# Eight wide matmuls and then eight narrow ones, in place of turns

## The chip, the cores and the metric

The kernel runs on one core of one Trainium2 chip. The metric is the device time of one execution in microseconds. The program is written in Python against a tile framework. Each engine (TensorE for matmuls, VectorE, ScalarE, GpSimd and SyncE) has a queue of its own, which it works off in order; a planner decides in which order the instructions enter the queues, from the order of the program, priorities and its own estimate of when things are ready, and it puts in the waits.

## The reference

The reference is one encoder layer over 512 positions of 2048 channels, in float32. A normed input is projected into two groups (a convolution module and a neighbourhood attention), these are normed and projected back, and a gated MLP follows. The part that matters here is the MLP's first step:

```python
xn = rms_norm(x, ffn_norm_g[l])
up = jnp.einsum("bsd,df->bsf", xn, w_up[l])          # (512 x 2048) by (2048 x 11264)
up = depthwise_conv(up, ffn_dw_w[l], ffn_dw_b[l])    # width 3
gate, val = jnp.split(up, 2, axis=-1)                # 5632 each
x = x + jnp.einsum("bsf,fd->bsd", jax.nn.silu(gate) * val, w_down[l])
```

## The kernel before

**Exactness.** TensorE is fed in a rounded 32-bit form. A float32 weight tile (`raw`, 128 x 1024, eight slices of 128 x 128) is split by `parts` into `whi`, a rounded copy that ScalarE makes (L125), and `wlo`, the remainder that VectorE makes (L126). Activations are split in the same way. A product is then the sum of three: high by high, high by low, low by high.

**Stages.** In order of time: the input projection (tiles `pj`, with the attention's matmuls between), the output projection (`po`), the up projection (`pu`, from about 702 to 1578 us) and the down projection (`pd`). `mm3` issues the three matmuls of a slice in turn (L138 and L141 with a slice of `whi`, L142 with the same slice of `wlo`). In the input and output projection all three have 512 columns. The down projection does its three at L819 to L821, each of 512 columns too, and there the weights are what moves.

**The up projection.** It works on 44 units `f` of 128 gate and 128 value columns. The 2 x 2 block product of a unit (halves of the channels by halves of the positions) is done with seven block products in place of eight, each with a sum or difference of weights and one of activations; `c` numbers them, and `TURN = (3, 2, 4, 5, 1, 0, 6)` is their order. The activations of all seven stand ready in `comb[c][k]`, for the eight slices k of 128 channels: a tile of 512 columns of which the first 256 (`H`) are the high part of the 256 positions and the last 256 the low part. So one matmul of `whi` with the whole tile gives high by high in the left half of the accumulator and high by low in the right half, and one matmul of 256 columns adds `wlo` by the high part to the left half. After the product, `folded` adds the halves (ScalarE L707, VectorE L708), or `copied` (ScalarE L704) copies the accumulator into another one on which a further product goes on.

Six of the seven products are made of these pairs, 16 matmuls each: L694 with 512 columns, L697 with 256. The product with c = 2 runs through `mm3` with halves of the tile, as 24 matmuls of 256 columns. An accumulator is one PSUM bank of 512 columns; a product's sixteen matmuls all add into the same one.

**What sets the order around it.** `weights()` is called at the start of a product; it makes the weights of the product three further on (`AHEAD = 3`, with `NW = 4` buffers for each of whi and wlo), which puts their loads on SyncE's queue, and up to eight products ahead (`FAR = 8`) it issues the two weight sums of a unit, as a load on SyncE's queue and an adding transfer on GpSimd's (L643). When all matmuls of a product are issued, `tick` lets pending steps follow the last one, and `done`, here `paced`, lets GpSimd issue transfers behind the last matmul of the fourth product (`ws`, sums of down weights, L191 and L194). `pin` keeps the first matmul of a product in the order of the program (from the second unit on); all others the planner places. The results of a unit pass through the width-3 convolution and the gate on ScalarE and VectorE, and go to DRAM for the down projection (L754) until the last units, which stay.

Of the kernel before, what the change touches and what calls it, by code (L numbers as in the profile page):

```python
# [16 lines left out]
P = 128  # L17
D = 2048
S = 512
# [15 lines left out]
U = 8  # L35
# [5 lines left out]
H = S // 2  # L41
# [31 lines left out]
def layer(ctx: ExitStack, tc: tile.TileContext, xT, xn, w_in, w_out, w_up, w_down, par, tab, g3, out):  # L73
    nc = tc.nc
# [8 lines left out]
    @contextmanager  # L83
    def shifted(by):

        at = tc.cur_priority
        tc.cur_priority = max(at + by, 0)
        yield
        tc.cur_priority = at + (tc.cur_priority - max(at + by, 0))

    def t2(name, dt=F32):
        return tp.tile([P, S], dt, tag="t2k", name=name)
# [17 lines left out]
    ps = psm.tile([P, S], F32, tag="mm", name="warm")  # L110
# [7 lines left out]
    def raw_unit(src, n):  # L118
        raw = t4([P, U * P], "raw")
        return raw, nc.sync.dma_start(raw[:, :n], src)  # L120

    def parts(raw, n):
        hi = wpool.tile([P, U * P], F32R, tag="whi", name="whi", bufs=NW)
        lo = wpool.tile([P, U * P], F32R, tag="wlo", name="wlo", bufs=NW)
        i = nc.scalar.activation(hi[:, :n], raw[:, :n], AF.Copy)  # L125
        j = nc.vector.tensor_sub(lo[:, :n], raw[:, :n], hi[:, :n].bitcast(F32))  # L126
        return hi, lo, i, j
# [5 lines left out]
    tight = []  # L133

    def mm3(ps, w, wk, mh, ml, start, stop, more=False):
        hi, lo = w[:2]
        a = slice(wk * P, (wk + 1) * P)
        i = nc.tensor.matmul(ps, hi[:, a], mh, start=start, stop=False, skip_group_check=more)  # L138
        if tight:
            pin(i)  # L140
        nc.tensor.matmul(ps, hi[:, a], ml, start=False, stop=False, skip_group_check=more)  # L141
        return nc.tensor.matmul(ps, lo[:, a], mh, start=False, stop=stop, skip_group_check=more)  # L142
# [4 lines left out]
    def tick(behind):  # L147
        for todo in (steps, asteps):
            while todo:
                try:  # L150
                    with tc.issue_after(behind.ins):
                        next(todo[0])
                    break
                except StopIteration:
                    todo.pop(0)
# [5 lines left out]
    def weights():  # L161
        at = weights.at
        weights.at += 1
        for i in range(at, min(at + 1 + FAR, len(plan))):
            if i in sums:
                sums.pop(i)()
        while len(made) < min(at + 1 + AHEAD, len(plan)):
            made.append(plan[len(made)]())
        return made[at]
# [81 lines left out]
    pin = tc.keep_in_program_order  # L251
# [24 lines left out]
    for j, n in enumerate((NC_, 0)):  # L276
        raw, i = raw_unit(w_in[n, :, U * P:2 * U * P], U * P)
        pin(i)
        w = parts(raw, U * P)
# [9 lines left out]
    for step in ORDER:  # L289
        i = next(a_ if step == "a" else q_)  # L290
# [238 lines left out]
    p, n = -1, 0  # L529
# [51 lines left out]
    comb = [[] for _ in range(7)]  # L581
# [103 lines left out]
    def up(f, done):  # L685

        def product(c, ps, more):
            hi, lo = wt = weights()
            for k in range(U):
                m, w = comb[c][k], slice(k * P, (k + 1) * P)  # L690
                if c == 2:
                    i = mm3(ps[:, :H], wt, k, m[:, :H], m[:, H:], k == 0, k == U - 1)
                    continue
                i = nc.tensor.matmul(ps, hi[:, w], m, start=k == 0 and not more, stop=False, skip_group_check=more)  # L694
                if k == 0 and tight:
                    pin(i)
                i = nc.tensor.matmul(ps[:, :H], lo[:, w], m[:, :H], start=False, stop=k == U - 1,  # L697
                                     skip_group_check=more)
            tick(i)
            done(TURN.index(c), i)  # L700

        def copied(to, ps):
            with shifted(-100):
                nc.scalar.activation(to, ps, AF.Copy)  # L704

        def folded(to, ps):
            nc.scalar.activation(to, ps[..., H:], AF.Copy)  # L707
            add(to, to, ps[..., :H])  # L708

        product(3, pa, False)  # L710
        tight[:] = [1] * (f > 0)
        copied(pd_, pa)
        product(2, pc_, False)
        w = t2("w")[:, :H]
        nc.scalar.activation(w, pc_[:, :H], AF.Copy)
        product(4, pa, True)
        copied(pe, pa)
        product(5, pd_, True)
        g = t2("g")
        folded(g[:, :H], pd_)  # L720
        product(1, pa, True)
        copied(pb, pa)
        product(0, pe, True)
        v = t2("vl")
        by = v.rearrange("p (i t) -> p i t", i=2)
        folded(by[:, 1], pa)
        folded(by[:, 0], pe)
        add(by, by, w.unsqueeze(1).broadcast_to([P, 2, H]))
        product(6, pb, True)
        folded(g[:, H:], pb)  # L730
        return g, v
# [269 lines left out]
```

## Time and profile before

| | us |
|---|---|
| median of 3 runs | 2015.14 (2013.87 to 2018.29) |
| the profiled execution | 2016.07 |
| its span, first to last instruction | 2014.3 |
| TensorE busy in it | 1994.4 |
| VectorE busy | 1599.6 |
| ScalarE busy | 1105.2 |
| mean granted TensorE clock | 0.997 |
| DMA moved | 451.01 MB, 224 GB/s |

The span is what the trace shows; what the execution took beyond it lies ahead of the first instruction and behind the last. In the profile PE stands for TensorE's matmuls, PEld for its weight loads, which run beside the matmuls, DVE for VectorE, ACT for ScalarE, POOL for GpSimd, SP for SyncE. Matmuls are pipelined: each is shown with a length that overlaps the next one's, so a matmul's price is the distance from its start to the next start. The chain of waits assigns every stretch of time on the path that ends last to one instruction, and for a stream of matmuls that is this distance.

### The profile page before, as it was taken

How to read it: one execution, taken by the hardware profiler on the slowest of the kernel's cores; microseconds unless marked ns; L12 is line 12 of the kernel's file. 1: busy time of each engine (PE TensorE's matmuls, PEld its weight loads, DVE VectorE, ACT ScalarE, POOL GpSimd, SP SyncE). 2: the span in 40 equal slices, each digit the busy share in tenths (PEclk: the TensorE clock that was granted, in tenths of full speed). 3: DMA queues.
4: the chain of work that ended last, by engine and by line, in shares of the span. 5: the costliest groups of instructions: out<-in, count | busy, mean ns of one | idle time of the engine just before them, and what ended most of it. 6: DMA issues, size and time to landing. Idle time of an engine off the chain costs nothing.

```text
span 2014.3 us, 28373 instructions
## 1 busy us (share of the span) xinstructions
PE 1994.4 (99%) x10525; PEld 1685.5 (84%) x10525; DVE 1599.6 (79%) x2296; ACT 1105.2 (55%) x1729; POOL 226.1 (11%) x310
## 2 busy tenths in 40 slices
PE   9999999999999999999999999999999999999998
PEld 7878888877788888888888888888888788888886
DVE  5994798498547888888888888888888798886765
ACT  7234423448525676666666666666666645554654
POOL 0110111110001111111111111111110400000000
PEclk9999999999999999999999999999999999999999
DMA  9677767776858879998999999999986976666563
GB/s 341 167 218 181 177 170 202 183 182 199 256 147 220 203 206 263 244 267 235 265 240 258 253 253 251 251 256 248 258 239 170 375 229 212 218 212 195 191 210 114
DMA packets 143114, 451.01 MB, mean 224 GB/s; under 512 B 15232, under 2 KB 23936, under 8 KB 141568
## 3 DMA queue, kind: packets, MB, share of 16 engines
q1 hardware_dynamic: 90608, 293.98, 43.6%
q0 software_dynamic: 42624, 148.92, 34.2%
q10 hardware_dynamic: 9744, 6.30, 1.0%
q8 instruction: 82, 1.34, 0.3%
q14 instruction: 56, 0.46, 0.1%
HBM read 430.27 MB, written 111.15 MB: 269 GB/s over the span
## 4 chain that ended last, share of the span: by engine, by line
PE 94%; DMA 2%; DVE 2%; ACT 1%; issue 0%; SPq 0%; DVEq 0%; ACTq 0%
PE pu L694 25%; PE pu L697 12%; PE pd L821 7%; PE pd L819 7%; PE pd L820 7%; PE pj L138 6%; PE pj L141 6%; PE pj L142 6%; PE po L138 3%; PE po L141 3%; PE po L142 3%; PE pu L141 2%; PE pu L138 2%; PE pu L142 2%; DVE y L367 1%; DMA xn<-in_xn 1%
## 5 line engine op out<-in xcount | busy, mean ns | idle before, releaser
L125 ACT ACTIVATE whi<-raw 128x1024 fp32r<-128x1024 f32 x572 | 605.5, 1059 | 722.4 <-PE pj L141 211.7
L126 DVE TENSOR_TENSOR wlo<-raw,whi 128x1024 fp32r<-128x1024 f32 x572 | 699.0, 1223 | 304.1 <-ACT whi L125 274.9
L694 PE MATMUL pu<-xc,whi 128*128 128x512 f32 x2112 | 748.2, 399 | 0.0
L697 PE MATMUL pu<-xc,wlo 128*128 128x256 f32 x2112 | 593.1, 281 | 0.0
L694 PEld LDWEIGHTS pu<-xc,whi 128*128 128x128 f32 x2112 | 396.8, 188 | 96.9 <-issue 0.2
L697 PEld LDWEIGHTS pu<-xc,wlo 128*128 128x128 f32 x2112 | 399.0, 189 | 0.3 <-issue 0.2
L138 PE MATMUL pj<-xh,whi 128*128 128x512 f32 x624 | 246.8, 398 | 1.4 <-DVE gate L352 1.4
L142 PE MATMUL pj<-xh,wlo 128*128 128x512 f32 x624 | 243.7, 390 | 0.8 <-DVE wlo L126 0.8
L141 PE MATMUL pj<-xl,whi 128*128 128x512 f32 x624 | 244.4, 392 | 0.1
L821 PE MATMUL pd<-whi,ho 128*128 128x512 f32 x616 | 240.1, 391 | 4.0 <-DVE ho L777 4.0
L819 PE MATMUL pd<-whi,ho 128*128 128x512 f32 x616 | 240.5, 391 | 0.5 <-ACT ho L776 0.5
L820 PE MATMUL pd<-wlo,ho 128*128 128x512 f32 x616 | 240.4, 390 | 0.0
L367 DVE SCALAR_TENSOR_TENSOR y<-ch,prm,y 128x507 f32<-128x507 f32 (+14 forms) x240 | 169.9, 742 | 3.2
L194 POOL DMA_DIRECT2D ws<-in_w_down x88 | 79.4, 902 | 568.1 <-DMA ws<-ws 279.0
L138 PEld LDWEIGHTS pj<-xh,whi 128*128 128x128 f32 x624 | 117.5, 188 | 30.2 <-issue 3.5
L821 PEld LDWEIGHTS pd<-whi,ho 128*128 128x128 f32 x616 | 116.0, 188 | 29.3 <-DVE ho L777 5.3
L142 PEld LDWEIGHTS pj<-xh,wlo 128*128 128x128 f32 x624 | 117.5, 188 | 26.1 <-DVE wlo L126 1.3
L141 PEld LDWEIGHTS pj<-xl,whi 128*128 128x128 f32 x624 | 117.7, 189 | 24.0 <-DVE xl L257 0.5
L819 PEld LDWEIGHTS pd<-whi,ho 128*128 128x128 f32 x616 | 115.9, 188 | 25.1 <-ACT ho L776 0.9
L820 PEld LDWEIGHTS pd<-wlo,ho 128*128 128x128 f32 x616 | 116.1, 188 | 24.6 <-DVE wlo L126 0.3
L643 POOL DMA_DIRECT2D raw<-in_w_up x88 | 85.2, 968 | 344.6 <-DMA raw<-in_w_up 85.6
L138 PE MATMUL pu<-xc,whi 128*128 128x256 f32 x352 | 99.7, 283 | 0.5 <-ACT xc L586 0.5
(185 smaller groups left out, 2524.4 us busy)
## 6 DMA issues: line engine op xcount, KB each, us to landing
raw<-in_w_up SPq DMA_DIRECT2D x220, 512.0 KB, 8.0
ws<-in_w_down POOLq DMA_DIRECT2D x132, 512.0 KB, 7.7
raw<-in_w_up POOLq DMA_DIRECT2D x88, 512.0 KB, 9.8
raw<-ws SPq DMA_DIRECT2D x88, 512.0 KB, 4.3
raw<-in_w_in SPq DMA_DIRECT2D x78, 512.0 KB, 5.1
raw<-in_w_down SPq DMA_DIRECT2D x66, 512.0 KB, 4.2
ws<-ws POOLq DMA_DIRECT2D x44, 512.0 KB, 7.9
raw<-in_w_out SPq DMA_DIRECT2D x32, 512.0 KB, 5.1
```

Of the source, the lines that this page charges most:

```text
L125: i = nc.scalar.activation(hi[:, :n], raw[:, :n], AF.Copy)
L126: j = nc.vector.tensor_sub(lo[:, :n], raw[:, :n], hi[:, :n].bitcast(F32))
L138: i = nc.tensor.matmul(ps, hi[:, a], mh, start=start, stop=False, skip_group_check=more)
L141: nc.tensor.matmul(ps, hi[:, a], ml, start=False, stop=False, skip_group_check=more)
L142: return nc.tensor.matmul(ps, lo[:, a], mh, start=False, stop=stop, skip_group_check=more)
L367: nc.vector.scalar_tensor_tensor(y[:, a:b], h[:, a + j - PAD:b + j - PAD], prm[:, o + j:o + j + 1], y[:, a:b], op0=ALU.mult, op1=ALU.add)
L643: nc.gpsimd.dma_start(a[c], w_up[f, q2], accum_op=ALU.add)
L694: i = nc.tensor.matmul(ps, hi[:, w], m, start=k == 0 and not more, stop=False, skip_group_check=more)
L697: i = nc.tensor.matmul(ps[:, :H], lo[:, w], m[:, :H], start=False, stop=k == U - 1, skip_group_check=more)
L819: nc.tensor.matmul(ps[i], h[:, t], wh[:, d], start=start and not more, stop=False, skip_group_check=more)
L820: nc.tensor.matmul(ps[i], h[:, t], wl[:, d], start=False, stop=False, skip_group_check=more)
L821: return nc.tensor.matmul(ps[i], h[:, tl], wh[:, d], start=False, stop=stop, skip_group_check=more)
```

## The change

Within each of the six products, all eight matmuls of 512 columns (with `whi`) come first, for k = 0 to 7, and then all eight of 256 columns (with `wlo`), where a 512 and a 256 for each k took turns before. The product with c = 2 stays as it is. The first 512 still opens the accumulation, and is still the pinned one; the last 256 still closes it and is the one that `tick` and `done` get. The number, shapes and operands of the matmuls stay.

```diff
         def product(c, ps, more):
             hi, lo = wt = weights()
-            for k in range(U):
-                m, w = comb[c][k], slice(k * P, (k + 1) * P)
-                if c == 2:
+            if c == 2:
+                for k in range(U):
+                    m = comb[c][k]
                     i = mm3(ps[:, :H], wt, k, m[:, :H], m[:, H:], k == 0, k == U - 1)
-                    continue
-                i = nc.tensor.matmul(ps, hi[:, w], m, start=k == 0 and not more, stop=False, skip_group_check=more)
-                if k == 0 and tight:
-                    pin(i)
-                i = nc.tensor.matmul(ps[:, :H], lo[:, w], m[:, :H], start=False, stop=k == U - 1,
-                                     skip_group_check=more)
+            else:
+                for part, n in ((hi, S), (lo, H)):
+                    for k in range(U):
+                        i = nc.tensor.matmul(ps[:, :n], part[:, k * P:(k + 1) * P], comb[c][k][:, :n],
+                                             start=part is hi and k == 0 and not more,
+                                             stop=part is lo and k == U - 1, skip_group_check=more)
+                        if part is hi and k == 0 and tight:
+                            pin(i)
             tick(i)
             done(TURN.index(c), i)
```

## The prediction

> **What bounds the kernel now.** I began with the profile's page: the busy table, the slices, and the costliest groups.
>
> ```profile
> span 2014.3 us, 28373 instructions
> PE 1994.4 (99%) x10525; PEld 1685.5 (84%) x10525; DVE 1599.6 (79%) x2296; ACT 1105.2 (55%) x1729; POOL 226.1 (11%) x310
> PEclk9999999999999999999999999999999999999999
> L694 PE MATMUL pu<-xc,whi 128*128 128x512 f32 x2112 | 748.2, 399 | 0.0
> L697 PE MATMUL pu<-xc,wlo 128*128 128x256 f32 x2112 | 593.1, 281 | 0.0
> ```
>
> TensorE is busy for 99% of the span at full granted clock, and the two groups that the change reorders have 2112 matmuls each, with no idle time in front of them. Their "mean ns of one" (399 and 281) overlap one another, so they are no prices: what counts is the spacing from one start to the next. I therefore went on to the table by stage, and for the up projection to the chain of waits and the groups of one stretch of it.
>
> ```profile
> 702.00:1000.00 298.00, 297.47 (x1800) 263.29 (x1799) 254.24 (x326) 189.25 (x279) 47.95 (x60) 1.00 0.90 245
> 1000.00:1300.00 300.00, 300.00 (x1817) 266.04 (x1815) 258.27 (x320) 187.55 (x272) 48.33 (x60) 1.00 0.93 254
> 1300.00:1578.00 278.00, 278.00 (x1684) 246.60 (x1683) 237.50 (x292) 173.46 (x251) 44.27 (x60) 1.00 0.86 240
> 1578.00:1620.00 42.00, 37.45 (x156) 29.61 (x155) 31.54 (x58) 22.71 (x43) 12.37 (x23) 0.96 0.95 354
> 1700.00:1900.00 200.00, 200.00 (x884) 165.62 (x883) 153.04 (x244) 103.69 (x156) 0.00 (x0) 1.00 0.65 203
> ```
>
> The columns are the stretch, its length, then busy time and count of PE, PEld, DVE, ACT and POOL, then the granted clock, DMA share and GB/s. From 702 to 1578 us (the up projection) TensorE has no gaps to speak of; VectorE is next, at 258 of 300 us. The stage is a stream of matmuls, so its length is the number of matmuls times their spacing. The chain of waits of the same 300 us, and the groups in it, give that spacing:
>
> ```profile
> by line: PE pu L694 56.9%; PE pu L697 28.8%; PE pu L142 4.8%; PE pu L141 4.8%; PE pu L138 4.8%
> L694 PE MATMUL pu<-xc,whi 128*128 128x512 f32 x728 | 257.7, 398 | 0.0
> L697 PE MATMUL pu<-xc,wlo 128*128 128x256 f32 x729 | 204.7, 281 | 0.0
> L142 PE MATMUL pu<-xc,wlo 128*128 128x256 f32 x120 | 34.0, 284 | 0.0
> L141 PE MATMUL pu<-xc,whi 128*128 128x256 f32 x120 | 34.0, 283 | 0.0
> L138 PE MATMUL pu<-xc,whi 128*128 128x256 f32 x120 | 34.0, 283 | 0.0
> ```
>
> All of the chain is TensorE. **In turns** a 512-column matmul takes 56.9% of 300 us over 728 = 234.5 ns, a 256-column one 28.8% over 729 = 118.5 ns, a pair 353.0 ns. The last three rows are the product with c = 2, which this stage already runs as 24 matmuls of 256 columns one after another: 4.8% of 300 us over 120 = **120.0 ns each in a run**.
>
> For 512-column matmuls in a run the down projection serves. The chain of 1700 to 1900 us:
>
> ```profile
> by line: PE pd L821 33.5%; PE pd L819 33.3%; PE pd L820 33.3%
> ```
>
> That is 100.1% of 200 us over the 884 matmuls of the table's row: **226.5 ns each in a run**. The timeline shows both rhythms matmul by matmul, turns first (start, length, instruction):
>
> ```profile
> 1199.92 0.40 PE L694 MATMUL pu<-xc,whi 128*128 128x512 f32 x1
> 1200.15 0.28 PE L697 MATMUL pu<-xc,wlo 128*128 128x256 f32 x1
> 1200.27 0.40 PE L694 MATMUL pu<-xc,whi 128*128 128x512 f32 x1
> 1200.51 0.28 PE L697 MATMUL pu<-xc,wlo 128*128 128x256 f32 x1
> 1200.63 0.40 PE L694 MATMUL pu<-xc,whi 128*128 128x512 f32 x1
> 1200.87 0.28 PE L697 MATMUL pu<-xc,wlo 128*128 128x256 f32 x1
> ...
> 1800.11 0.39 PE L820 MATMUL pd<-wlo,ho 128*128 128x512 f32 x1
> 1800.34 0.39 PE L821 MATMUL pd<-whi,ho 128*128 128x512 f32 x1
> 1800.57 0.39 PE L819 MATMUL pd<-whi,ho 128*128 128x512 f32 x1
> ```
>
> A 512-column matmul followed by a 256-column one holds the engine for 0.23 to 0.24 us, one followed by its like for 0.23 us: the 8 ns lie at the edge of this view's rounding, so the sum goes by the chain.
>
> **The change, part by part.** No matmul, weight load, transfer or byte is added or removed. Six of the seven products of each of the 44 units change, 2112 / 8 = 264 products.
>
> (1) Spacing of the 512-column matmuls. Before, each of a product's eight is followed by a 256-column one. After, seven are followed by their like and one by a 256-column one. Seven times (226.5 - 234.5) = -56 ns a product. The bounds of this price are 226.5 (the run in the down projection) and 234.5 (what they take in this stage now). I take the lower, because type, shape and the weight tiles of eight slices are alike, and because it is also what the input projection has under a busier VectorE, from a stretch of its chain:
>
> ```profile
> 182.21 0.23 PE pj L141
> 182.44 0.23 PE pj L142
> 182.66 1.06 PE sc L453 x8
> 183.73 1.02 PE trp L481 x8
> ```
>
> (2) Spacing of the 256-column ones. Seven of eight are now followed by another 256: 7 x (120.0 - 118.5) = +10.5 ns. The nearest row from below is the eight transposes of 128 columns above, 1.02 us over 8 = 128 ns with their entry, which is no lower than 120, so the low end is the 118.5 of the turns. From above, the row below: one weight load lasts 189 ns, and if none of what a run of 256-column matmuls cannot cover were hidden the spacing would be that. I take 120.0, since it was measured in this stage on these operands.
>
> ```profile
> L697 PEld LDWEIGHTS pu<-xc,wlo 128*128 128x128 f32 x728 | 137.5, 189 | 0.0
> ```
>
> (3) The two changes of width. One 512 to 256 and one 256 to 512 are left in each product, at 234.5 and 118.5 as now. Sum of a product: before 8 x 353.0 = 2824 ns; after 7 x 226.5 + 234.5 + 7 x 120.0 + 118.5 = 2778.5 ns. **Saved: 45.5 ns, times 264 = 12.0 us.**
>
> The Trainium skill bears on exactly this. In "TensorE: Matmul & The Clock Gate", section "Back-to-back issue gap", the gap of a warm isolated matmul is its columns over 2.4 plus 2.5 ns, whatever stands next to it; the section "LDWEIGHTS" puts a load at its columns over 1.2, 107 ns for 128. By both, estimated, a pair costs 216 + 109 ns in any order and the change saves nothing. The same section says that in a real stream of loads and matmuls both ops set the spacing, so the Trainium skill leaves room for the other outcome. The trace does not agree with order being indifferent: a 512 costs 234.5 before a 256 and 226.5 before a 512, as quoted above.
>
> (4) When weights are needed and given back. The first use of a product's wlo moves from its second matmul to its ninth, 7 x 226.5 = 1.6 us later; its last use of whi starts 7 x 226.5 = 1.59 us into the product in place of 7 x 353.0 = 2.47 us, 0.9 us earlier. Who waits for whom in the stage, 710 to 1570 us:
>
> ```profile
> POOL ws L194 <- DMA ws<-ws: 186.6, 20, 10.4
> ACT whi L125 <- PE pu L694: 161.8, 172, 1.5
> DVE wlo L126 <- ACT whi L125: 112.4, 87, 1.8
> ACT vl L707 <- PE pu L697: 47.4, 43, 1.1
> PEld pu L694 <- issue: 0.2, 1, 0.2
> ```
>
> ScalarE waits 161.8 us for TensorE to give whi back, TensorE for nobody. An earlier whi lets ScalarE convert earlier and VectorE follow; nothing on the path is late because of it, so I cost it at nothing. The cover is the head start of the weights (three products, `AHEAD`). If ScalarE's instructions come out in another order, the copies between accumulators have a whole product, 2.8 us, before TensorE needs them.
>
> (5) What hangs on a product's last matmul. `tick`, the DMAs that `paced` gives POOL, and ScalarE's and VectorE's reading of the accumulator (L707 waits for L697, above) hang on the same matmul as before, which ends 45.5 ns sooner. `weights()`, which puts five loads on SP's queue and two adding transfers on POOL's per unit, is called at the same place. No DMA passes another.
>
> (6) A faster stage asks for the same bytes in 1.4% less time (12.0 of 876 us): 254 GB/s becomes 258. The 354 GB/s of the stretch after 1578 us shows that there is room; with the cover gone, the loss is bounded by the gain.
>
> (7) The stretch 1578 to 1620 us, where TensorE stands still for 4.6 us, is set off by the last unit's products and moves forward with them. At worst seven products' saving of cover, 7 x 45.5 = 0.3 us.
>
> The profiled execution took 2016.07 us, 2014.3 of it the span; less 12.0 it gives 2004.1. It lies 0.93 us above the median of 2015.14, and from that median the same sum gives **2003.1**, which I round to 2003.
>
> **The rivals.**
>
> *The order does not matter* (chance 0.06): the 8 ns belong to this stage, where DMA is busy for 0.93 and VectorE for 258 of 300 us, and not to the turns. Then the 512s stay at 234.5 and only the +10.5 ns of (2) come: 264 x 10.5 = +2.8 us, 2018, inside what I call no change. If widths alone set the pace it is 2015. For it: no run of 512s stands in this stage. Against it: the c = 2 run, in this very stage, differs from the turns by 1.5 ns only and the other way, and 512s take 0.23 us at 182 us too. The gap formula of the Trainium skill would come out as this rival.
>
> *A run of 256s is bound by its weight loads* (0.06, slower): in the c = 2 product two of three loads in a row fetch the same slice of whi, in the new run each fetches a fresh one. If a fresh load can't hide behind 120 ns, the spacing goes up towards the 189 ns of the load's row: 264 x 7 x (189 - 120) = +127.5 us on 2003, about 2131 us. It decides from 45.5 / 7 = 6.5 ns a matmul, so from 126.5 ns on. Against it: the three rows of that product have the same 4.8%, though L138 and L142 load fresh slices and L141 a repeated one.
>
> *The planner places ScalarE's and VectorE's work otherwise* (0.03, slower): whi ready sooner in its reckoning may put a conversion in front of a copy that TensorE needs; one such stall of 0.2 us a unit would cost 44 x 0.2 = 8.8 us of the 12.0, and from 0.3 us a unit the sign turns. No row shows TensorE waiting now.
>
> *More than the sum* (0.05): runs at 226.5 and 118.5, and nothing lost at the two changes of width (226.5 and 118.5): 2824 - 8 x 345.0 = 64 ns, 16.9 us, 1998.
>
> **How the numbers follow.** The forecast has 0.80, the greater gain 0.05: faster 0.85. The sum that fails in part, a 512 at 230 in this stage, half-way between its bounds, saves 264 x 21 ns = 5.5 us, 2009.6, and is inside the forecast's own range of 1999 to 2010. About 0.2% (4 us) is what a measurement of this kernel can tell from no change. Same: 0.06. Slower: 0.09. The range that leaves out no more than 2 in 10 reaches from the greater gain to just short of no change: 1998 to 2011.
>
> **What would show it.** In the changed profile: L694's successor in turns gone, the timeline giving one group of eight 512s every 1.8 us and then eight 256s in about 1 us; the chain of 300 us in the up projection with some 226 to 228 ns a 512 and 120 ns a 256; the up projection 12 us shorter, all else as long as now; ScalarE's whi waits for L694 ended sooner. I would be wrong if the 256s' spacing passes 126 ns, if the 512s stay at 234, or if TensorE shows waits inside the stage.

## The result and the profile after

| | before | after |
|---|---|---|
| median | 2014.86 us (20 runs, 2012.79 to 2021.22) | 2008.78 us (20 runs, 2007.12 to 2014.88) |
| profiled execution | 2016.07 us, span 2014.3 | 2010.19 us, span 2008.4 |

The ratio is 0.9969, with a 95% interval of 0.9961 to 0.9976: about 6.2 us faster (4.8 to 7.9), half of the 12.0 that were forecast. The forecast of 2003 was 5.8 us too low, and the time is inside the range. Lines have moved: L696 of the changed kernel is L694 and L697 of the one before.

From the changed kernel's page:

```profile
span 2008.4 us, 28339 instructions
PE 1984.2 (99%) x10525; PEld 1685.5 (84%) x10525; DVE 1598.6 (80%) x2296; ACT 1097.4 (55%) x1729; POOL 226.1 (11%) x310
L696 PE MATMUL pu<-xc,whi 128*128 128x512 f32 x2112 | 529.8, 392 | 0.2 <-ACT pu L706 0.2
L696 PE MATMUL pu<-xc,wlo 128*128 128x256 f32 x2112 | 294.5, 282 | 0.0
```

The busy times of the two groups fell from 748.2 and 593.1 us, but this is a matter of the overlap: before, each matmul lapped over one of the other group. The spacing tells what was won. The chain of waits from 1000 to 1300 us now names one line for all six products (start, length, what):

```profile
by line: PE pu L696 85.7%; PE pu L138 4.8%; PE pu L141 4.8%; PE pu L142 4.8%
1009.39 16.76 PE pu L696 x96
1029.03 16.76 PE pu L696 x96
```

From one stretch of 96 to the next it is 1029.03 - 1009.39 = **19.64 us a unit**, and six products of 16 take 16.76 us, 2793 ns each. Before, the c = 2 product of two successive units began here (timeline):

```profile
1204.51 0.28 PE L138 MATMUL pu<-xc,whi 128*128 128x256 f32 x1
...
1224.34 0.28 PE L138 MATMUL pu<-xc,whi 128*128 128x256 f32 x1
```

That is 19.83 us a unit. So 0.19 us a unit is won where 6 x 45.5 ns = 0.27 were forecast. In the trace every unit from the second on takes 19.64 us, with no exception.

Where the rest went can be seen in the changed kernel's timeline. The first three rows give a product; the others are answers for stretches that begin one matmul later each, so that their starts show the eight wide matmuls one by one:

```profile
1199.00 1.11 PE L696 MATMUL pu<-xc,wlo 128*128 128x256 f32 x8
1199.95 2.00 PE L696 MATMUL pu<-xc,whi 128*128 128x512 f32 x8
1201.79 0.40 PE L696 MATMUL pu<-xc,wlo 128*128 128x256 f32 x2
...
1200.18 1.77 PE L696 MATMUL pu<-xc,whi 128*128 128x512 f32 x7
1200.42 1.53 PE L696 MATMUL pu<-xc,whi 128*128 128x512 f32 x6
1200.65 1.31 PE L696 MATMUL pu<-xc,whi 128*128 128x512 f32 x5
1200.88 1.07 PE L696 MATMUL pu<-xc,whi 128*128 128x512 f32 x4
1201.11 0.84 PE L696 MATMUL pu<-xc,whi 128*128 128x512 f32 x3
1201.34 0.62 PE L696 MATMUL pu<-xc,whi 128*128 128x512 f32 x2
```

The eight narrow ones take 1199.95 - 1199.00 = 0.95 us (forecast 958.5 ns), the eight wide ones 1201.79 - 1199.95 = 1.84 us (forecast 1820 ns). In the trace's nanoseconds the wide ones are spaced **233, 236, 228, 233, 231 and only then 227, 227, 227**, and the narrow ones 113, 119 and then 120. The wide run has to settle: the first five lose 27 ns against five times 226.7. The same settling stands in the trace of before, in the input projection, where wide matmuls follow those of the attention:

```profile
247.85 0.50 PE L138 MATMUL pj<-xh,whi 128*128 128x512 f32 x1
248.19 0.40 PE L141 MATMUL pj<-xl,whi 128*128 128x512 f32 x1
248.42 0.39 PE L142 MATMUL pj<-xh,wlo 128*128 128x512 f32 x1
248.65 0.40 PE L138 MATMUL pj<-xh,whi 128*128 128x512 f32 x1
248.88 0.39 PE L141 MATMUL pj<-xl,whi 128*128 128x512 f32 x1
```

After the first (0.34 us) they are 0.23 us apart here too, and in the trace's nanoseconds 236, 228, 233, 231 and then 227: the same numbers in the same order. (Other runs there begin otherwise; the last section has them.) The prediction took the price of a wide matmul from a stretch of 200 us without a break, which doesn't show how a run begins.

The second part of the loss lies in the first unit. What TensorE waited for from 640 to 730 us, after the change (the two longest of three):

```profile
PE trx L594 <- DVE x L603: 3.0, 1, 3.0
PE pu L138 <- ACT xc L586: 1.4, 1, 1.4
```

Before it was the second alone, with 0.5 us. TensorE's order around it, before and then after:

```profile
709.05 0.38 PE L138 MATMUL pu<-xc,whi 128*128 128x256 f32 x1 [0.53 <-ACT xc L586]
709.28 0.50 PE L694 MATMUL pu<-xc,whi 128*128 128x512 f32 x1
709.62 0.28 PE L697 MATMUL pu<-xc,wlo 128*128 128x256 f32 x1
...
710.39 0.38 PE L138 MATMUL pu<-xc,whi 128*128 128x256 f32 x1 [1.36 <-ACT xc L586]
710.61 0.50 PE L696 MATMUL pu<-xc,whi 128*128 128x512 f32 x1
710.95 1.12 PE L696 MATMUL pu<-xc,wlo 128*128 128x256 f32 x8
```

The wait is for the activations of the eighth slice, the last to be made. Before, seven of the first product's eight narrow matmuls were done ahead of it and one was left behind it; now all eight stand behind it.

By the trace's starts, the two profiled executions differ by 5.9 us of span: 43 units at -0.187 make -8.0, the first unit takes 24.4 in place of 23.0 us (+1.4), the up projection begins 1.3 us later, and what follows it is 0.6 us shorter.

### The profile page after: what moved, and what is told of

Its sections match the earlier page's. It is cut to its first block, busy times and chain, and to the rows that moved or that the text cites. A ratio compares the mean times of both kernels' runs of the same rounds, so it can differ in the third digit from the quotient of the medians.

```text
span 2008.4 us, 28339 instructions
## 1 busy us (share of the span) xinstructions
PE 1984.2 (99%) x10525; PEld 1685.5 (84%) x10525; DVE 1598.6 (80%) x2296; ACT 1097.4 (55%) x1729; POOL 226.1 (11%) x310
## 4 chain that ended last, share of the span: by engine, by line
PE 93%; DMA 3%; DVE 2%; ACT 1%; issue 1%; SPq 0%; DVEq 0%; ACTq 0%
PE pu L696 37%; PE pd L823 7%; PE pd L821 7%; PE pd L822 7%; PE pj L138 6%; PE pj L141 6%; PE pj L142 6%; PE po L138 3%; PE po L141 3%; PE po L142 3%; PE pu L141 2%; PE pu L142 2%; PE pu L138 2%; DVE y L367 1%; DMA xn<-in_xn 1%; DMA x<-in_xT 1%
## 5 line engine op out<-in xcount | busy, mean ns | idle before, releaser
L125 ACT ACTIVATE whi<-raw 128x1024 fp32r<-128x1024 f32 x572 | 605.5, 1059 | 709.9 <-PE pj L141 207.3
L696 PE MATMUL pu<-xc,whi 128*128 128x512 f32 x2112 | 529.8, 392 | 0.2 <-ACT pu L706 0.2
L696 PEld LDWEIGHTS pu<-xc,whi 128*128 128x128 f32 x2112 | 379.9, 189 | 68.7 <-issue 0.5
L696 PEld LDWEIGHTS pu<-xc,wlo 128*128 128x128 f32 x2112 | 288.1, 190 | 20.5
L696 PE MATMUL pu<-xc,wlo 128*128 128x256 f32 x2112 | 294.5, 282 | 0.0
L822 PEld LDWEIGHTS pd<-wlo,ho 128*128 128x128 f32 x616 | 116.0, 188 | 24.4 <-DVE wlo L126 0.3
```

The costliest lines, as they stand in the source:

```text
L696: i = nc.tensor.matmul(ps[:, :n], part[:, k * P:(k + 1) * P], comb[c][k][:, :n], start=part is hi and k == 0 and not more, stop=part is lo ...
L822: nc.tensor.matmul(ps[i], h[:, t], wl[:, d], start=False, stop=False, skip_group_check=more)
```

## The experiments

What was open: whether the settling belongs to the break between widths, to a new product with its weights and its accumulator, or to weight loads that a 256-column matmul can hardly cover; and whether the two waits at the change of stage come from the planner's order or from chance.

**The first unit in turns.** All units but the first stay as after the change.

```diff
+                wide, narrow = [(hi, S, k) for k in range(U)], [(lo, H, k) for k in range(U)]
+                r = U if f else 1
+                todo = [x for a in range(0, U, r) for x in wide[a:a + r] + narrow[a:a + r]]
```

(The loop then issues `todo` in order, the first matmul opening the accumulation and pinned, the last one closing it. All edits below are of this `todo`.)

> The first of the 44 units keeps its turns, the other 43 have eight wide (512-column) and then eight narrow (256-column) matmuls. Theory (the regrouped first unit made the planner place VectorE's, ScalarE's and TensorE's work at the change of stage otherwise, and this cost 2.8 us): the wait of 3.0 us before the transposes at 699 us and that of 1.4 us at 709 us go, the first matmul of the up projection is back at 702.9 us, a unit in the middle stays at 19.64 us, and the time is 43 x 0.187 = 8.0 us under before, ratio 0.9960. Rival (the 2.8 us are chance of one profiled run): the waits come again somewhere, and the time is 6.0 us under before, ratio 0.9970.

Measured: ratio 0.9962 (0.9949 to 0.9974), median 2007.95 us. The profiled span was 2005.0 us, a unit stayed at 19.64 us, the first took 22.8 us, and TensorE's waits from 640 to 730 us were those of before:

```profile
PE pu L138 <- ACT xc L586: 0.5, 1, 0.5
```

So the longer wait comes from the order in which the planner placed the first unit, and its size can be worked out: each narrow matmul that is no longer ahead of the wait, at 120 ns, brings TensorE to the wait that much earlier. Seven of them add 0.84 us to 0.53, and the trace has 1.36. The runs of two and of four below, whose first unit is regrouped as well, leave one and three more behind the wait, which gives 0.65 and 0.89; their traces have 0.65 and 0.88. The wait accounts for 0.8 of the 1.4 us by which the first unit grew; the rest lies in the third wait of 0.15 us and in slower matmuls, and was not taken apart further. For the total, 7.7 us (5.2 to 10.3) agree with the 8.0, but the interval does not part them from the changed kernel's 6.2.

**Runs of 16 across products.**

```diff
+                todo = narrow + wide if c in (4, 1, 6) else wide + narrow
```

> Products 4, 1 and 6 take their narrow matmuls first and then the wide ones, so that runs of 16 like matmuls stand across the borders of products and a unit has 3 stretches of wide ones in place of 6. Theory (each time that wide matmuls follow narrow ones the first five are slower by 27 ns in all, and the first two narrow ones after wide ones faster by 7.5, a loss of 20 ns a round): a unit falls from 19.64 to 19.58 us, the time by 2.6 us against the changed kernel, 8.8 under before, ratio 0.9956; the second product's wide matmuls of a stretch hold 226.7 ns from the first on. Rival (the slow start goes with a new product, its weight tiles or its accumulator, whatever stood ahead): a unit stays at 19.64 us and each product's first five wide ones stay slow, ratio 0.9969.

Measured: the timeline of a unit, and its chain from 1000 to 1300 us:

```profile
1006.93 3.82 PE L697 MATMUL pu<-xc,whi 128*128 128x512 f32 x16
1010.59 2.08 PE L697 MATMUL pu<-xc,wlo 128*128 128x256 f32 x16
1012.50 3.82 PE L697 MATMUL pu<-xc,whi 128*128 128x512 f32 x16
```

```profile
1006.14 16.70 PE pu L697 x96
1025.72 16.70 PE pu L697 x96
```

A unit takes 1025.72 - 1006.14 = 19.58 us, as the theory said. Sixteen wide ones take 1010.59 - 1006.93 = 3.66 us, which is 16 x 226.7 plus 27 ns once; the second product's eight hold 226.7 ns from the first on, with another weight tile and another accumulator. The settling goes with the break in the run, and the rival falls. The time was 2009.67 us, ratio 0.9970 (0.9959 to 0.9981), above the forecast 0.9956; the profiled execution took the least of the six, 2005.85 us. The edit does what it should in the stage, but the gain isn't to be seen in the total. The other five took 2009.22 to 2011.77 us, at a mean granted clock of 0.994 to 0.997 where the profiled one had 0.997, and the lowest clock is that of the longest; a lower clock thus goes with part of it, and what else they had, no trace shows.

**Both edits.**

> Both of these edits. If both theories hold they add: 43 units x (19.827 - 19.58) = 10.6 us under before, 2004.3 us at a before of 2014.9, ratio 0.9947. If neither holds 0.997.

Measured: 19.58 us a unit, 23.0 us the first, ratio 0.9957 (0.9943 to 0.9970), median 2006.69 us: 8.7 us (6.0 to 11.5), in whose interval the 10.6 of the forecast lie. The profiled execution had a wait of 1.7 us ahead of the transposes at 699 us, although the first unit was as before.

**Runs of four.**

```diff
+                r = 4
+                todo = [x for a in range(0, U, r) for x in wide[a:a + r] + narrow[a:a + r]]
```

> Runs of four wide and four narrow matmuls, two of each in a product. Theory (a settling that goes by the place in the run: wide 233.3, 235.8, 228.4, 232.5, then narrow 113.3, 119.2, 120, 120): 1402.5 ns a run of eight, 2805 a product, 19.71 us a unit. Rival (a fixed price of 20 ns for every round of widths): 2773.3 + 40 = 2813 ns a product, 19.76 us a unit. Without any price of rounds it would be 2773 ns and 19.52 us.

Measured: 16.84 us for six products in the chain, 2807 ns each, 19.72 us a unit, near the theory's 2805 and not the rival's 2813. But only the first wide run of a product followed the places (233, 236, 228, 233); the second went 235, 233, 236, 224, the first narrow run 117, 119, 118, 117 in place of 113, 119, 120, 120, and the second 117, 120, 120, 120. That the sum came out right with much of its terms wrong is luck. The one execution took 2010.12 us.

**Runs of two.** As before, with `r = 2`.

> Runs of two wide and two narrow matmuls. Theory (the settling goes by the place in the run): 233.3 + 235.8 + 113.3 + 119.2 = 701.6 ns for two pairs, 2806 ns a product, 19.72 us a unit, as with runs of four. Rival (the loss falls evenly with the length of the run from 53 ns a product in turns): about 2800 ns.

Measured, the timeline and the chain:

```profile
1000.32 0.39 PE L698 MATMUL pu<-xc,wlo 128*128 128x256 f32 x2
1000.55 0.62 PE L698 MATMUL pu<-xc,whi 128*128 128x512 f32 x2
1001.01 0.40 PE L698 MATMUL pu<-xc,wlo 128*128 128x256 f32 x2
...
1025.28 16.72 PE pu L698 x96
```

A product takes 16.72 / 6 = 2787 ns, less than with runs of eight (2793) or four (2807), against 2824 in turns. The wide ones of a product are at 233, 236, 233, 231 ns, but the narrow ones at 116, 113, 113, 119, so that two pairs take 697 ns where two settled pairs take 693. Both expectations fall: what a break costs is no function of the place in the run, nor does it fall evenly with the length. The one execution took 2005.91 us, and the first unit 22.9.

**Narrow matmuls of 384 columns.**

```diff
-                wide, narrow = [(hi, S, k) for k in range(U)], [(lo, H, k) for k in range(U)]
+                wide, narrow = [(hi, S, k) for k in range(U)], [(lo, 3 * P, k) for k in range(U)]
```

> The changed kernel with 384 columns in place of 256 in each matmul of wlo: for 128 of the 256 positions it adds the product of the low parts, which the kernel leaves out. Theory A (the slow first five belong to narrow matmuls whose 120 ns are close to the length of a weight load): at 173.3 ns no such thing is left, the wide ones hold 226.7 ns from the first on, a product takes 8 x 226.7 + 8 x 173.3 = 3200 ns. Theory B (any change of width or other break of a run starts a settling anew): the first five wide ones are slow by some 27 ns in all, a product takes about 3220 ns. The time is 107 us above the changed kernel's either way, about 2116 us.

Measured: 2130.96 us. Six products take 19.58 us, 3264 ns each. Of one of the five whose wide matmuls come behind 384s:

```profile
1008.28 2.01 PE L698 MATMUL pu<-xc,whi 128*128 128x512 f32 x8
1010.13 1.58 PE L698 MATMUL pu<-xc,wlo 128*128 128x384 f32 x8
1011.54 2.01 PE L698 MATMUL pu<-xc,whi 128*128 128x512 f32 x8
```

Theory A falls: behind narrow matmuls with 53 ns more to cover each load, the wide ones take 1.85 us, not 8 x 226.7 = 1.81, and the 384s 1.41 us in place of 8 x 173.3 = 1.39. Theory B has the direction, but the loss is 64 ns a product, not 20: in these five the wide ones do not settle within eight (229, 233, 236, 224, 231, 236, 228, 233), and the 384s go through 175, 175, 178, 185, 176, 182 before they hold 173. In the sixth, behind the 256-column matmuls of c = 2, the wide ones go through 233, 236, 228, 232, 231 and then 227 as in the changed kernel. So the longer narrow matmul made the break dearer here, and the time is 122 us above the changed kernel's, not 107.

**The changed kernel again.** No edit.

> The changed kernel once more, as a mate of the others. Theory (the 1.4 us before the eighth slice of the first unit is the planner's order, the 3.0 us ahead of the transposes at 699 us was a late transfer of that run): unit 0 takes 24.4 us again (23.0 before the change), the 3.0 us wait does not come again or comes with another length, the span is 2005 to 2008 us. Rival (both belong to the order): both come again as they were. Ratio 0.9967 either way.

Measured: ratio 0.9967 (0.9955 to 0.9978), median 2008.73 us, span 2007.0. TensorE's waits from 640 to 730 us:

```profile
PE pu L138 <- ACT xc L586: 1.4, 1, 1.4
```

The 1.4 us came again, as they did with the runs of 16, and the 3.0 us did not. In the first profile of the changed kernel, ScalarE stood behind a transfer just before:

```profile
ACT xc L586 <- DMA xt<-xt: 3.3, 1, 3.3
```

This is a write of transposed activations to DRAM that landed late in that execution. In this profile of the same program ScalarE waited for it too, 2.3 us but at another instruction (L211), and TensorE did not stand still; so TensorE's wait of 3.0 us belongs to the execution, not to the order alone. With both edits ScalarE waited 2.0 us for it and TensorE 1.7. The kernel before had 0.2 us of it in its one profile, and five of the nine profiles of changed kernels have 2.0 to 3.8; whether the new order makes it likelier stays open. The expectation of 24.4 us for the first unit did not hold, it was 26.8 us, for a reason that the table by stage shows (columns as in the prediction, the clock third from the end):

```profile
708.00:711.00 3.00, 3.00 (x20) 2.92 (x21) 2.24 (x9) 2.77 (x8) 0.00 (x0) 0.78 1.04 162
711.00:714.00 3.00, 3.00 (x9) 2.42 (x9) 2.90 (x7) 1.25 (x2) 0.00 (x0) 0.50 0.28 59
```

The granted clock was 0.50 from 711 to 714 us, and only nine matmuls, eight of them wide, fall into these 3 us. The first profile of the changed kernel, with the same 1.4 us and the 3.0 us besides, had 1.00 there.

**All seven products wide and narrow.** Both edits, and c = 2 in the same form from the second unit on.

```diff
-            if c == 2:
+            if c == 2 and f == 0:
...
-        nc.scalar.activation(w, pc_[:, :H], AF.Copy)
+        if f:
+            folded(w, pc_)
+        else:
+            nc.scalar.activation(w, pc_[:, :H], AF.Copy)
```

> The kernel with both edits (first unit as before the change, runs of 16), and from the second unit on the product c = 2 as eight wide and eight narrow matmuls as well, in place of 24 narrow ones; its halves are folded by ScalarE and VectorE. Theory (226.7 ns wide, 120 narrow, 20 a round of widths, four rounds a unit): 7 x 2773.3 + 4 x 20 = 19.49 us a unit, 43 x (19.827 - 19.493) = 14.3 us under before, ratio 0.9929. Rival (the added fold, 0.36 us of ScalarE and 0.41 us of VectorE a unit, or the later release of the accumulator makes TensorE wait): a unit of 19.58 us or more, ratio 0.995 or more.

Measured: ratio **0.9941** (0.9928 to 0.9954), median 2004.53 us, below both kernels: the interval also lies below the 0.9961 to 0.9976 of the changed one. The chain and the table of 1000 to 1300 us, and TensorE's waits from 640 to 1570 us:

```profile
by line: PE pu L699 100.1%
999.91 300.19 PE pu L699 x1725
```

```profile
1000.00:1300.00 300.00, 300.00 (x1726) 264.98 (x1725) 266.71 (x341) 189.40 (x277) 49.69 (x62) 1.00 0.96 257
```

```profile
PE trx L594 <- DVE x L603: 3.5, 1, 3.5
PE pu L138 <- ACT xc L586: 0.5, 1, 0.5
```

A unit is 112 matmuls now, and 300.19 us over 1725 is 174.0 ns, 19.49 us a unit, as forecast: 0.33 us less than before, 14.3 us over 43 units. VectorE carries the fold (266.71 of 300 us) and TensorE waits for nobody inside the stage once its first unit is done, so the rival falls. The total shows 11.9 us (9.3 to 14.5), in whose interval the 14.3 lie. In the profiled execution a wait of 3.5 us fell ahead of the transposes, and the granted clock was 0.50 from 705 to 708 us, so that the first unit took 23.7 us.

## Why the prediction was half right

- **Direction and mechanism right.** Matmuls of two widths in turns cost more than in runs, in a stage that is nothing but their spacing. Neither *the order does not matter* nor *a run of 256s is bound by its weight loads* came about: the narrow run holds 120 ns, the very price that (2) took from the c = 2 product, though each load is of a fresh slice.
- **(1) is the term that was mis-sized.** "Seven times (226.5 - 234.5) = -56 ns": the 226.5 came from a steady run, and a run of eight spends its first five on settling. The eight wide ones take 1841 ns in place of 1820. On the other side, (2) and (3) were too dear: the first narrow one is at 113 ns, not 120, and the last wide one at 227, not 234.5; the eight narrow ones take 952 in place of 958.5. The product takes 2793 ns in place of 2778.5; 264 x 15 ns = 3.9 us of the 12.0. The case in which the sum fails in part, a wide one at 230 ns, is what came about: 1841 / 8 = 230.1. That its 2009.6 us lie so near the 2008.78 measured is in part luck: the stage won 8.0 us, not the 5.5 of that case, and the first unit gave some back.
- **234.5 and 118.5 are not distances between starts.** By the trace's starts, the 512s in turns from 1000 to 1300 us are spaced 236.1 ns and the 256s 116.9. The chain divides the time by the matmuls' ends, and these are modelled. In a run of like matmuls the two agree, and the pair of 353.0 ns is right either way, and with it the sum; only its split between (1), (2) and (3) was off by 1.6 ns a matmul.
- **The planner's order cost something, but not as its rival had it.** That rival was given 0.03 and put as a stall in every unit, by ScalarE's and VectorE's work; what the trace has is TensorE's own order, once: the first unit is 1.4 us longer, 0.8 of it the wait, since the order of its first two products decides how TensorE meets the last activations of the stage before. (4) and (7) looked at the middle and at the end of the stage, and not at its beginning, where activations are still being made.
- **Together.** 43 units x 0.187 = 8.0 us, less 1.4 of the first unit, is 6.6 us; measured are 6.2 (4.8 to 7.9).
- **(4), (5), (6) held.** No wait for weights, buffers or POOL appeared on TensorE in the middle of the stage, and DMA moved 256 GB/s from 1000 to 1300 us (258 were expected):

```profile
1000.00:1300.00 300.00, 300.00 (x1833) 269.17 (x1832) 260.48 (x322) 186.24 (x274) 48.63 (x61) 1.00 0.93 256
```

- ScalarE's waits after the change, from 710 to 1570 us:

```profile
ACT whi L125 <- PE pu L696: 119.4, 91, 1.5
ACT vl L709 <- PE pu L696: 81.7, 43, 1.9
```

- Its wait for whi on these matmuls fell from 161.8 to 119.4 us, as (4) said, but others took most of the place: all its waits ahead of L125 fell from 249.5 to 237.2 us only, and the one for the accumulator (L707, now L709) rose from 47.4 to 81.7. None of it reached TensorE.
- **The rule of the Trainium skill** that was weighed there ("TensorE: Matmul & The Clock Gate", section "Back-to-back issue gap") gives the gap of an isolated matmul by its width alone. In this stream width alone does not give it: the same 2112 wide and 2112 narrow matmuls took 2824, 2807, 2787 and 2793 ns a product in runs of one, four, two and eight.

## What to carry to other kernels

Where TensorE's stream is the bound, try like matmuls in runs against widths that alternate: every run length tried here was cheaper than turns (2783 to 2807 ns a product against 2824), and a run may cross from one product into the next if the accumulators allow it. Longer was not steadily better, so measure more than one length. Price a matmul not from the middle of a steady stretch alone but from the first ones after a break, which the trace of the old kernel often has somewhere. And look at the first pass of a reordered loop by itself: that is where its inputs are still on their way and where the planner's order decides.

## What the runs showed that had not been expected

- How a wide run begins depends on what stood ahead of it. Behind eight or more 256-column matmuls it goes through 233, 236, 228, 233, 231 ns and then holds 227, in every unit of the changed kernel from the second on. In the input projection of the kernel before, behind the attention's matmuls and a longer first one, it goes 236, 228, 233, 231 at 247.85 us, holds 227 from the second on at 151.78 us, and goes 229, 233, 236, 224, 231, 236, 228, 233 at 184.50 us, which is the series behind 384-column matmuls. In turns nothing settled: most of the stage repeats 236, 232, 241 for the wide ones and 113, 118, 120 for the narrow.
- So a round of widths has no fixed price. Above the settled 8 x 226.7 + 8 x 120.0 = 2773 ns a product, it costs 6 ns in turns, 3 in runs of two, 17 in runs of four, and 20 in runs of eight and of 16; with 384-column matmuls the loss is 64 ns a product.
- The settled spacings, 226.7, 173.3 and 120.0 ns for 512, 384 and 256 columns, lie 53.3 and 53.3 ns apart, which is 13.3 ns and 0.417 ns a column. What sets the unsettled ones stays open; the runs rule out a new weight tile, a new accumulator, and loads that a 256-column matmul just fails to cover. Nor is it the change between whi and wlo: the c = 2 product makes it at one width and holds 120 ns after the change.
- The c = 2 product, not edited, took 121, 120, 124, 118, 117 ns in a repeating order before, without settling in 24 matmuls, and 120 flat after the change; its mean stayed at 120.
- The half clock of 3 us and more, behind a wait of 1.4 us in one of two profiles of the same kernel and around the wait of 3.5 us with all seven products in runs, and a late transfer that holds TensorE up by 1.7 to 3.5 us in three of the profiles, are of the size of what was to be measured. One profiled span says little about a change of 0.3%; the repeated unit of the loop, exact to 0.01 us, says much.
